# Three PSUM banks for dense products and one for heads, value differences on GpSimd, and weight casts that are deferred and kept in program order

## The chip, the cores and the metric

The kernel runs on one core of one Trainium2 chip. TensorE (PE in the profile) multiplies, VectorE (DVE), ScalarE (ACT) and GpSimd (POOL) work on tiles, and SyncE (SP) issues most DMAs. The metric is the device time of one execution in microseconds (us); lower is better.

## What is computed

A trunk of two layers on a sequence of 2048 tokens with 1024 channels, in float32:

```python
# layer 0
h = rms_norm(x, a_norm[i])
u, z = jnp.split(h @ a_w_in[i], 2, axis=-1)
# pooled: trailing means of u over 2, 4, 8, 16 tokens (one width per 256 channels) minus u
mixed = jnp.einsum('bsgc,gcd->bsgd', pooled, w_group) * scale
x = x + (mixed * jax.nn.silu(z)) @ a_w_out[i]
x = x + (p[i] @ ple_w[i]) * jax.nn.sigmoid(x @ ple_gate_w[i])
# once
k_all, v_all = jnp.split(rms_norm(x, kv_norm) @ w_kv, 2, axis=-1)
k_sh, v_sh = rms_norm(split_heads(k_all), k_norm), split_heads(v_all)
# layer 1
q, z = jnp.split(rms_norm(x, b_norm[j]) @ b_w_in[j], 2, axis=-1)
o = stick_breaking_attention(rms_norm(split_heads(q), b_q_norm[j]), k_sh, v_sh)  # 16 heads of 64, strictly causal
x = x + (o * jax.nn.silu(z)) @ b_w_out[j]
x = x + (p[i] @ ple_w[i]) * jax.nn.sigmoid(x @ ple_gate_w[i])
```

In the attention, beta = sigmoid(q·k/8), and a key's share is its beta times the product of (1 - beta) over the keys between it and the query. The kernel gets that product with a scan along the keys, and sums it against differences of neighbouring rows of v, which are therefore computed ahead ("value differences").

## The kernel before

Every operand of a product is held as a rounded high part and a low part (the rest), side by side in one tile, and a product is three matmuls: high by high, low by high, high by low. A high part is a cast or a scaled copy on ScalarE; the low part is a subtraction on VectorE or GpSimd. So each weight is loaded raw, cast (`put_split`, L183 or, where a norm's gain goes in, L189) and completed (L185, L190) before its products can start, and each activation that comes out of a product goes through `split` (L165, L166).

The tokens go in four chunks of 512. There are two streams of work. The **dense stream** (`stream`) is a generator that makes one step (three matmuls in most places) at a time: mixer, output projection (`out_steps`, whose sum with the residual is L600), the gate with its embedding (`gate_steps`: sigmoid L634, product L637, sum L638), the projections to q, k and v (`kvq`) and the gate z of layer 1 (`gate_z`). The **attention** of a chunk runs over slots of one head and one block of 512 keys: `front` (logits into psl banks, sigmoid L920, scan L924), `turn` three half-slots later (transposes into psa banks, cast L939 and low part L941) and `gather` four half-slots later (product with the value differences into a pso bank). `gather` ends a head: ScalarE copies one half of the bank out (L956), VectorE adds the other half (L957), and for every second head `gated` adds the last row (L964), multiplies by the gate on GpSimd (L965), splits and stores.

The program has three parts. `boot()` and `until((0, 0))` run the dense stream alone up to the first chunk's queries (a part called solo below: dense products rotate over the banks psd, psl and pso). Then 44 dense steps and the main loop follow: each of its turns emits one gather, turn and front, and then `fill` makes as many dense steps as a fixed rate says. Last, the projection and gate of the last chunk run alone. PSUM's eight banks are two each of psd (dense), psl (logits), pso (heads) and psa (transposes).

What sets the order: PE keeps the program's order after the mark (0, 0). On the other engines a scheduler orders instructions by its own timeline, except those that `tc.keep_in_program_order` holds behind the one traced before them. ScalarE takes its instructions strictly one after the other, so one that waits holds back those behind it. Helper `late(n, ...)` has its calls made n dense steps later (`after(n, ...)` and `store(n, ...)` likewise), and `lag` is a list of pieces that `kvq` takes up later, one at a time. Raw weights, inputs and gates share four tiles with the tag io. Nine weight pairs (`UNITS`) are in use or on their way at a time.

The value path is: `valued` scales the product (vr, L690), stores it, loads it back shifted by one row (vs); `differences` subtracts (L707, GpSimd), casts the high part (vv, L710, ScalarE), makes the low part (L711, VectorE) and stores both to DRAM (vd), from where a head's tile is loaded (L898). The path of q and k is: `keyed` scales (qs, L718), squares (sqq, L720), reduces (L723), and a piece in `lag` transposes and splits (hl, L737 to L739). A head's query tile qb is qa with its halves swapped, two copies on ScalarE (L887).

Of the kernel before, what the change touches and what calls it, by code (L numbers as in the profile page):

```python
# [37 lines left out]
def trunk_kernel(ctx, tc, x, p, a_norm, wu_t, wz_a, w_group, a_scale, a_w_out, kv_norm, w_kv,  # L38
# [90 lines left out]

    io = flat("io", 4)  # L130
    tmp_ = lambda nm: pool.tile([P, HALO + W5], F32, tag="tmp", name=nm, bufs=6)
# [47 lines left out]
    held = deque()  # L179

    def put_split(pr, raw, kts, gain):
        if gain is None:
            A.copy(out=pr[:, 0], in_=raw)  # L183
            state["lo"] += 1
            (G if state["lo"] % 3 and not state["boot"] else V).tensor_tensor(out=pr[:, 1], in0=raw, in1=f(pr[:, 0]), op=ALU.subtract)  # L185
            return
        for i, kt in enumerate(kts):
            g = gain[:, kt : kt + 1]
            booted(A.activation(out=pr[:, 0, i], in_=raw[:, i], func=AF.Identity, scale=g))  # L189
            booted(V.scalar_tensor_tensor(out=pr[:, 1, i], in0=raw[:, i], scalar=g, in1=f(pr[:, 0, i]),  # L190
                                          op0=ALU.mult, op1=ALU.subtract))

    def unit(key, src, kts, n, gain, keep):
        kk = len(kts)
        pr = pool.tile([P, 2, kk, n], F32R, tag="wpair", name="wpair", bufs=UNITS)
        if key in once:
            nc.sync.dma_start(out=f(pr), in_=once[key])
            return pr, kts
        raw = io("wraw").rearrange("q (k n) -> q k n", k=kk)
        booted(nc.sync.dma_start(out=raw, in_=src[:, kts[0] : kts[-1] + 1]))  # L200

        def finish():
            put_split(pr, raw, kts, gain)
            if keep:
                store(70, out=once[key], in_=f(pr))

        if keep:
            once[key] = scratch(f"once{len(once)}", [P, 2, kk, n])
        if state["boot"]:
            later.append(finish)  # L210
        else:
            finish()
        return pr, kts

# [65 lines left out]
    def product(ps, us, acts, c0, back):  # L280
        n = len(acts)
        i = 0
        for u, kts in us:
            for e, kt in enumerate(kts):
                hi, lo = (u[:, l, e, c0 : c0 + P] for l in range(2))
                T.matmul(ps, hi, acts[kt][:, 0], start=(i == 0), stop=False)
                yield
                T.matmul(ps, hi, acts[kt][:, 1], start=False, stop=False)
                yield
                i += 1  # L290
                T.matmul(ps, lo, acts[kt][:, 0], start=False, stop=(i == n))
                if back and e == len(kts) - 1:
                    give_back()
                yield

    def product2(pss, us, acts):
# [3 lines left out]
        for part, back in ((us[:-1], False), (us[-1:], True)):  # L300
            for k in range(2):
                for u, kts in part:
                    for e, kt in enumerate(kts):
# [184 lines left out]


    def silu(ps, rb):  # L490
        zr, sg = tmp("zr"), tmp("sg")
        V.tensor_tensor(out=zr, in0=ps, in1=rb, op=ALU.mult)
        A.activation(out=sg, in_=zr, func=AF.Sigmoid)
        G.tensor_tensor(out=zr, in0=zr, in1=sg, op=ALU.mult)
        return zr
# [150 lines left out]
    for j in (0, 2):  # L646
        STEPS += [(j, kt) for kt in range(4)]
        STEPS += [(j + i, kt + 4 * (1 - i)) for kt in range(4) for i in (1, 0)]
        STEPS += [(j + 1, kt) for kt in range(4, KT)]

    def kvq(s, kind, b):
        ck = chunk[s]
        us = take(KT)
        banks, early = {}, []
        for j, kt in STEPS:
            tk = slice(j * P, (j + 1) * P)
            if kt == 0:
                banks[j] = dense()
            u = us[kt][0]
            for xh, wh in ((0, 0), (1, 0), (0, 1)):  # L660
                T.matmul(banks[j], ck["x2"][kt][:, xh, tk], u[:, wh, 0], start=(kt == 0 and xh == wh),
# [11 lines left out]
            if "r2" not in ck:  # L673
# [32 lines left out]
    def differences(s, b, j, vr, vs):  # L706
        G.tensor_tensor(out=vs, in0=vs, in1=vr, op=ALU.subtract)  # L707
        vs = vs.rearrange("q (h d) -> q h d", d=HD)
        vv = t4("vv").rearrange("q l (h d) -> q (l h d)", d=HD).rearrange("q (h l d) -> q h l d", l=2, d=HD)
        late(10, lambda: A.copy(out=vv[:, :, 0, :], in_=vs),  # L710
             lambda: V.tensor_tensor(out=vv[:, :, 1, :], in0=vs, in1=f(vv[:, :, 0, :]), op=ALU.subtract))  # L711
        store(22, out=vd[s][b][:, :, j, :].rearrange("h q n -> q h n"),
              in_=f(vv).rearrange("q h e d -> q h (e d)"))
# [54 lines left out]
    def gate_z(s):  # L768
        ck = chunk[s]

        def put(o, zr):
            sg = tmp("sg")
            A.activation(out=sg, in_=zr, func=AF.Sigmoid)
            G.tensor_tensor(out=zr, in0=zr, in1=sg, op=ALU.mult)
            store(20, out=zd[s][o], in_=zr)

        first = []
        if "r2" in ck:
            ck["rb2"] = bcast(ck["r2"], "y")
        else:  # L780
            us = take(4)
# [148 lines left out]

    def turn(st, kt):
        j0 = kt if st["diag"] else 0
        pt = bank("psa", "psa")
# [9 lines left out]
    def gather(st, kt):  # L943
        cs = slice((kt if st["diag"] else 0) * P, W5)
        if st["diag"] and kt == 0:
            st["o"].append(bank("pso", "pso"))
        if st["last"] and kt == 1 and st["h"] % 2:
            st["zt"] = io("zt")
            nc.sync.dma_start(out=st["zt"], in_=zd[st["c"]][st["h"] // 2])
        po, at, vv = st["o"][0], st["at"].pop(kt), st["v"]  # L950
        T.matmul(po[:, cs], vv[:, kt, :], at[:, 0, cs], start=(st["diag"] and kt == 0), stop=False)
        T.matmul(po[:, cs], vv[:, kt, :], at[:, 1, cs], start=False, stop=(st["last"] and kt == 3))
        if st["last"] and kt == 3:
            half, os, c, h2 = st["h"] % 2, st["os"], st["c"], st["h"] // 2
            mine, other = slice(half * HD, (half + 1) * HD), slice((1 - half) * HD, (2 - half) * HD)
            A.copy(out=os[mine], in_=po[other])  # L956
            V.tensor_tensor(out=os[mine], in0=po[mine], in1=os[mine], op=ALU.add)  # L957
            if half:
                gated(c, h2, os, st["zt"])

    def gated(c, h2, os, zt):
# [4 lines left out]
        pr = t4("op")  # L966
        split(pr, os, G)
        if (c, h2) == (NSUB - 1, KT - 1):
            last["pair"] = pr
        else:  # L970
            store(20, out=od[c][h2], in_=f(pr))

# [33 lines left out]
    begin(0)  # L1006
    for _ in range(44):
        next(run)
    owed = 0.0
    count = 0  # L1010
# [113 lines left out]
```

## Time and profile before

| | us |
|---|---|
| median of 3 runs | 2738.69 (2737.61 to 2740.13) |
| the profiled execution | 2737.53 |
| its span, first to last instruction | 2735.7 |
| TensorE's weight loads, busy (beside matmuls) | 2248.6 |
| DMA engines, mean rate over the span | 247 GB/s |
| dense matmuls into psd, two largest groups, busy | 563.1 and 555.6 |

The span's page is from the profiled execution. Its rows by line give busy time, the mean of one instruction in ns, and the idle time just before them with what ended it. The rows of waits give the engine, the instruction that waited, after "<-" the one that released it, and then the total, the count and the longest in us. A row of the timeline starts with the start time, then the duration, and in brackets the idle time before with its releaser. The rows that matter are in the prediction.

### The profile page before, as it was taken

To read this page: it belongs to the slowest core of one execution; us is meant where nothing else is said; L and a number is where in the kernel's file an instruction comes from. 1 tells how busy PE (TensorE), PEld (TensorE's weight loads), DVE (VectorE), ACT (ScalarE), POOL (GpSimd) and SP (SyncE) were. 2 spreads that over 40 slices of the span, in tenths; PEclk is the share of its full clock that TensorE was granted. 3 is DMA by queue.
4 is the path that set the end of the run, shared out by engine and by line. 5 is a ranking of instruction groups with operands and counts; after the bars stand their busy time and mean duration, and the time that the engine had idled before them with its cause. 6 is when DMAs were issued, how large, how long until landed. Compare 5 with 4: busy or idle time off the path is not lost.

```text
span 2735.7 us, 38014 instructions
## 1 busy us (share of the span) xinstructions
PE 2688.5 (98%) x13406; PEld 2248.6 (82%) x13406; DVE 1786.0 (65%) x2303; ACT 1307.9 (48%) x2606; POOL 845.6 (31%) x681
## 2 busy tenths in 40 slices
PE   9999989999999999999999999999999999999999
PEld 7878778888787888888878888888888888888887
DVE  6736454644355866665568878766778778787742
ACT  5335553334556434564554445554565445444431
POOL 1345543324533423373333212232222102011102
PEclk9999999999999999999999999999999999999999
DMA  7789878676889878689796565677586666657545
GB/s 267 267 280 353 293 245 284 205 256 235 284 317 321 288 234 282 227 294 360 244 324 203 198 220 178 231 274 235 173 268 211 233 208 205 208 198 249 192 156 183
DMA packets 304410, 675.81 MB, mean 247 GB/s; under 512 B 46430, under 2 KB 79198, under 8 KB 304220
## 3 DMA queue, kind: packets, MB, share of 16 engines
q1 hardware_dynamic: 303644, 672.59, 72.0%
q8 instruction: 106, 1.74, 0.3%
q10 hardware_dynamic: 576, 0.79, 0.1%
q14 instruction: 84, 0.69, 0.1%
HBM read 485.05 MB, written 188.22 MB: 246 GB/s over the span
## 4 chain that ended last, share of the span: by engine, by line
PE 80%; DMA 5%; DVE 3%; ACT 2%; POOL 2%; issue 2%; SPq 1%; ACTq 0%; DVEq 0%; POOLq 0%
PE psd L47 53%; PE pso L47 9%; PE psl L47 9%; PE psa L51 8%; DVE pp L924 1%; PE pst L51 1%; DMA xin<-in_x_dram 1%; DMA vs<-vraw 1%; DMA wraw<-in_w_kv_dram 1%; DVE at L941 1%; SPq L66 1%; DMA wpair<-once 1%; DMA wraw<-in_gate_a_dram 1%; POOL rq L158 0%; DVE us L508 0%
## 5 line engine op out<-in xcount | busy, mean ns | idle before, releaser
L924 DVE TENSOR_TENSOR_SCAN pp<-pp,floor 128x512 f32<-128x512 f32 (+3 forms) x640 | 748.0, 1204 | 6.0 <-ACT pp L920 4.4
L941 DVE TENSOR_TENSOR at<-psa,at 128x512 fp32r<-128x512 f32 (+3 forms) x640 | 361.5, 605 | 344.8 <-ACT at L939 343.2
L47 PE MATMUL psd<-wpair,x 128*128 128x512 f32 x2304 | 563.1, 395 | 7.0 <-ACT qs L718 3.3
L47 PE MATMUL psd<-x,wpair 128*128 128x512 f32 x2304 | 555.6, 392 | 8.9 <-ACT sg L634 4.0
L939 ACT CAST at<-psa 128x512 fp32r<-128x512 f32 (+3 forms) x640 | 302.8, 524 | 533.8 <-PE psa L51 531.6
L47 PEld LDWEIGHTS psd<-x,wpair 128*128 128x128 f32 x2304 | 432.4, 189 | 104.0 <-ACT sg L634 6.1
L47 PEld LDWEIGHTS psd<-wpair,x 128*128 128x128 f32 x2304 | 427.1, 189 | 97.7 <-ACT qs L718 4.7
L47 PE MATMUL psd<-xp,wpair 128*128 128x512 f32 x1536 | 362.4, 391 | 3.0 <-DMA wpair<-once 1.4
L47 PEld LDWEIGHTS psd<-xp,wpair 128*128 128x128 f32 x1536 | 286.0, 188 | 64.9 <-DMA wpair<-once 1.9
L47 PE MATMUL pso<-at,vv 128*128 128x512 f32 (+3 forms) x1280 | 314.2, 365 | 6.7 <-DVE at L941 4.4
L920 ACT ACTIVATE pp<-psl 128x512 f32<-128x512 f32 (+3 forms) x640 | 316.1, 550 | 2.6 <-PE psl L47 2.1
L51 PE MATMUL psa<-ident,pp 128*128 128x128 f32 x2176 | 291.9, 274 | 0.8 <-ACT rby L366 0.8
L47 PEld LDWEIGHTS pso<-at,vv 128*128 128x128 f32 x1280 | 231.3, 188 | 58.5 <-DVE at L941 7.8
L51 PEld LDWEIGHTS psa<-ident,pp 128*128 128x128 f32 x2176 | 253.0, 141 | 29.5 <-ACT rby L366 1.0
L47 PE MATMUL psl<-kk,qa 128*128 128x512 f32 (+3 forms) x640 | 257.3, 407 | 0.0
L47 PE MATMUL psl<-kk,qb 128*128 128x512 f32 (+3 forms) x640 | 233.5, 365 | 6.0 <-ACT qb L887 6.0
L47 PE MATMUL psd<-og,wpair 128*128 128x512 f32 x744 | 182.2, 391 | 2.1 <-DVE os L957 1.4
L47 PE MATMUL psd<-mp,wpair 128*128 128x512 f32 x768 | 179.3, 390 | 0.0
L47 PEld LDWEIGHTS psd<-mp,wpair 128*128 128x128 f32 x768 | 143.8, 188 | 30.1
L47 PEld LDWEIGHTS psd<-og,wpair 128*128 128x128 f32 x744 | 138.8, 188 | 32.8 <-DVE os L957 1.8
L965 POOL TENSOR_TENSOR os<-os,zt 128x512 f32<-128x512 f32 x32 | 50.5, 1577 | 346.1 <-ACT os L964 264.7
L627 POOL TENSOR_TENSOR xj<-x 128x512 f32<-128x512 f32 x64 | 106.7, 1671 | 141.7 <-DVE sg L638 133.7
(121 smaller groups left out, 2825.7 us busy)
## 6 DMA issues: line engine op xcount, KB each, us to landing
wpair<-once SPq DMA_DIRECT2D x468, 512.0 KB, 5.1
once<-wpair SPq DMA_DIRECT2D x116, 512.0 KB, 5.8
kk<-kd SPq DMA_DIRECT2D x160, 256.0 KB, 3.7
vv<-vd SPq DMA_DIRECT2D x160, 256.0 KB, 3.9
wpair<-wf SPq DMA_DIRECT2D x48, 512.0 KB, 6.2
once<-kp SPq DMA_DIRECT2D x36, 512.0 KB, 5.5
qd<-hl SPq DMA_DIRECT2D x64, 256.0 KB, 4.4
qa<-qd SPq DMA_DIRECT2D x64, 256.0 KB, 4.5
```

The source lines that it names most:

```text
L47: return held_in_order(nc.tensor.matmul(*a, **k))
L51: return held_in_order(nc.tensor.transpose(*a, **k))
L66: after(n, lambda: nc.sync.dma_start(**k))
L627: G.tensor_tensor(out=xj, in0=f(x1[o][:, 0]), in1=f(x1[o][:, 1]), op=ALU.add)
L920: A.activation(out=pp[:, r0:], in_=ps[:, :w], func=AF.Sigmoid, scale=-1.0)
L924: V.tensor_tensor_scan(out=pp[:, r0:][:, ::-1], data0=pp[:, r0:][:, ::-1], data1=least, initial=1.0 if st["diag"] else st["carry"][j], op0 ...
L939: A.copy(out=at[:, 0, cs], in_=pt[:, cs])
L941: return lambda: V.tensor_tensor(out=at[:, 1, cs], in0=pt[:, cs], in1=f(at[:, 0, cs]), op=ALU.subtract)
L965: G.tensor_tensor(out=os, in0=os, in1=zt, op=ALU.mult)
```

## The change

- **Banks.** psd gets three banks and pso one. In the solo part dense products rotate over psd, psl, pso, psd, psl, psd.
- **Head copies.** ScalarE copies out both halves of a head's bank (the new tile is own, line 986 of the changed kernel), and VectorE adds from SBUF.
- **Value differences.** The high part is a copy on GpSimd and the low part a subtraction there, both six steps later (before: ten); the store is 24 steps later (before 22).
- **Weight casts.** After the boot part, a raw weight's cast is made five steps after its load was issued, or when a product first needs it, or when its io tile is to be used again (`settle`); and every such cast, with the kept ones (kp), stays in program order on ScalarE.
- **Sigmoids of the z gates** come five steps later (`gated_late`).
- **Order of steps.** Of the first chunk's first projection, two row blocks go weight by weight (`FIRST_STEPS`). The broadcast of the second norm goes into `lag` for chunks 1 to 3. The load of a head pair's gate zt goes from `gather` to `turn`. A head pair's split is 12 steps later and its store at 34. The first head's qb copies come after 24 of the 44 steps, in place of the first slot.

```diff
-    io = flat("io", 4)
+    io_ = flat("io", 4)
+    ring = deque([None] * 4, maxlen=4)
+
+    def io(nm, owner=None):
+        if ring[0] is not None:
+            settle(ring[0])
+        ring.append(owner)
+        return io_(nm)
...
-        return psum.tile([P, W5], F32, tag=tag, name=nm)
+        return psum.tile([P, W5], F32, tag=tag, name=nm, bufs={"psd": 3, "pso": 1}.get(tag, 2))
...
-        return bank(("psd", "psl", "pso")[state["turn"] % 3], "psd")
+        return bank(("psd", "psl", "pso", "psd", "psl", "psd")[state["turn"] % 6], "psd")
...
+    held_split = tc.keep_in_program_order
+
     def put_split(pr, raw, kts, gain):
         if gain is None:
-            A.copy(out=pr[:, 0], in_=raw)
+            held_split(A.copy(out=pr[:, 0], in_=raw))
...
-            booted(A.activation(out=pr[:, 0, i], in_=raw[:, i], func=AF.Identity, scale=g))
+            held_split(A.activation(out=pr[:, 0, i], in_=raw[:, i], func=AF.Identity, scale=g))
...
         else:
+            unsplit[id(pr)] = finish
+            after(5, lambda: settle(pr))
+        return pr, kts
+
+    unsplit = {}
+
+    def settle(pr):
+        finish = unsplit.pop(id(pr), None)
+        if finish:
             finish()
-        return pr, kts
...
+    def gated_late(zr, sg):
+        n = 0 if state["solo"] else 5
+        late(n, lambda: A.activation(out=sg, in_=zr, func=AF.Sigmoid))
+        after(n, lambda: G.tensor_tensor(out=zr, in0=zr, in1=sg, op=ALU.mult))
+        if not n:
+            pass_time(0)
...
+    FIRST_STEPS = [(j, kt) for kt in range(KT) for j in range(2)] + STEPS[16:]
...
+                if s:
+                    lag.append((time["now"] + 20, lambda: ck.update(rb2=bcast(ck["r2"], "y"))))
...
-        late(10, lambda: A.copy(out=vv[:, :, 0, :], in_=vs),
-             lambda: V.tensor_tensor(out=vv[:, :, 1, :], in0=vs, in1=f(vv[:, :, 0, :]), op=ALU.subtract))
-        store(22, out=vd[s][b][:, :, j, :].rearrange("h q n -> q h n"),
+        after(6, lambda: G.tensor_copy(out=vv[:, :, 0, :], in_=vs))
+        after(6, lambda: G.tensor_tensor(out=vv[:, :, 1, :], in0=vs, in1=f(vv[:, :, 0, :]), op=ALU.subtract))
+        store(24, out=vd[s][b][:, :, j, :].rearrange("h q n -> q h n"),
...
+        if st["last"] and kt == 0 and st["h"] % 2:
+            st["zt"] = io("zt")
+            nc.sync.dma_start(out=st["zt"], in_=zd[st["c"]][st["h"] // 2])
...
+            own = tmp("own")
             A.copy(out=os[mine], in_=po[other])
-            V.tensor_tensor(out=os[mine], in0=po[mine], in1=os[mine], op=ALU.add)
+            A.copy(out=own[mine], in_=po[mine])
+            V.tensor_tensor(out=os[mine], in0=own[mine], in1=os[mine], op=ALU.add)
...
-        split(pr, os, G)
+        split(pr, os, G, 12)
...
-    for _ in range(44):
+    for i in range(44):
         next(run)
+        if i == 24:
+            active[0]["q"][2]()
```

VectorE's order at the end of the first chunk's output projection, before: L600 adds the residual to a product (the eighth of this projection is xr_1951), L185 completes a weight, L166 is an activation's low part. Numbers behind names are tile numbers.

```order
L600 TENSOR_TENSOR xr_1861<-psd_1902,xr_1861 128x512
L166 TENSOR_TENSOR x1_1954<-xr_1861,x1_1954 128x512
L185 TENSOR_TENSOR wpair_1933<-wraw_1934,wpair_1933 128x512
L600 TENSOR_TENSOR xr_1896<-psd_1957,xr_1896 128x512
L185 TENSOR_TENSOR wpair_2009<-wraw_2010,wpair_2009 128x512
L600 TENSOR_TENSOR xr_1951<-psd_1990,xr_1951 128x512
L166 TENSOR_TENSOR x1_2040<-xr_1951,x1_2040 128x512
```

And now (L626 is the former L600, L195 the former L185, L174 the former L166):

```order
L626 TENSOR_TENSOR xr_1859<-psd_1900,xr_1859 128x512
L174 TENSOR_TENSOR x1_1952<-xr_1859,x1_1952 128x512
L195 TENSOR_TENSOR wpair_1933<-wraw_1934,wpair_1933 128x512
L626 TENSOR_TENSOR xr_1894<-psd_1955,xr_1894 128x512
L626 TENSOR_TENSOR xr_1949<-psd_1989,xr_1949 128x512
L174 TENSOR_TENSOR x1_2038<-xr_1949,x1_2038 128x512
L195 TENSOR_TENSOR wpair_2009<-wraw_2010,wpair_2009 128x512
```

The last sum, now xr_1949, and the low part of its split stand ahead of weight 2009's low part, no longer behind it.

ScalarE's order ahead of the first head's swapped query, before: L710 are casts of value differences, L189 weight casts, L718 and L720 a projection's scaled rows and their squares, L887 the two copies to qb.

```order
L189 ACTIVATE wpair_3821<-wraw_3822,gains_106 128x512
L189 ACTIVATE wpair_3832<-wraw_3833,gains_106 128x512
L710 CAST vv_3767<-vs_3706 128x8x64
L189 ACTIVATE wpair_3843<-wraw_3844,gains_106 128x512
L189 ACTIVATE wpair_3854<-wraw_3855,gains_106 128x512
L718 ACTIVATE qs_3862<-psd_3792,r_2674 128x512
L720 ACTIVATE sqq_3864<-qs_3862 128x512
L189 ACTIVATE wpair_3876<-wraw_3877,gains_106 128x512
L189 ACTIVATE wpair_3884<-wraw_3885,gains_106 128x512
L718 ACTIVATE qs_3905<-psd_3817,r_2674 128x512
L720 ACTIVATE sqq_3907<-qs_3905 128x512
L887 COPY qb_3813<-qa_3812 64x512 x2
```

And now (L199 is the former L189, L749 and L751 the former L718 and L720, L915 the former L887):

```order
L751 ACTIVATE sqq_3782<-qs_3780 128x512
L199 ACTIVATE wpair_3821<-wraw_3822,gains_106 128x512
L199 ACTIVATE wpair_3832<-wraw_3833,gains_106 128x512
L199 ACTIVATE wpair_3843<-wraw_3844,gains_106 128x512
L749 ACTIVATE qs_3860<-psd_3791,r_2657 128x512
L751 ACTIVATE sqq_3862<-qs_3860 128x512
L199 ACTIVATE wpair_3854<-wraw_3855,gains_106 128x512
L915 COPY qb_3812<-qa_3811 64x512 x2
L199 ACTIVATE wpair_3878<-wraw_3879,gains_106 128x512
L199 ACTIVATE wpair_3884<-wraw_3885,gains_106 128x512
L749 ACTIVATE qs_3903<-psd_3816,r_2657 128x512
```

The copies to qb passed two weight casts and a pair of qs and sqq, and the cast of value differences ahead of them left ScalarE.

ScalarE's order in the solo part, where the second half of the values' weights is cast, now: L397 copies a norm's sums (the former L377), L768 and L769 copy and cast transposed keys (the former L737 and L738), L721 scales values (the former L690). Before, the casts of these two weights (wpair_3593 and wpair_3618 there) stood ahead of all of these rows.

```order
L397 COPY ss_3549<-pst_3544 128x4
L768 ACTIVATE hl_3577<-pst_3572 128x512
L721 ACTIVATE vr_3654<-psd_3558,r_2657 128x512
L721 ACTIVATE vr_3699<-psd_3588,r_2657 128x512
L769 CAST hl_3577<-hl_3577 128x512
L768 ACTIVATE hl_3602<-pst_3597 128x512
L769 CAST hl_3602<-hl_3602 128x512
L199 ACTIVATE wpair_3592<-wraw_3593,gains_106 128x512
L199 ACTIVATE wpair_3617<-wraw_3618,gains_106 128x512
```

The two weight casts went behind them.

More of the change, by code (lines that the diff above doesn't have):

```diff
@@ L198, in unit @@
             return pr, kts
-        raw = io("wraw").rearrange("q (k n) -> q k n", k=kk)
+        raw = io("wraw", pr).rearrange("q (k n) -> q k n", k=kk)
         booted(nc.sync.dma_start(out=raw, in_=src[:, kts[0] : kts[-1] + 1]))
@@ L492, in silu @@
         V.tensor_tensor(out=zr, in0=ps, in1=rb, op=ALU.mult)
-        A.activation(out=sg, in_=zr, func=AF.Sigmoid)
-        G.tensor_tensor(out=zr, in0=zr, in1=sg, op=ALU.mult)
+        gated_late(zr, sg)
         return zr
@@ L654, in kvq @@
         banks, early = {}, []
-        for j, kt in STEPS:
+        for j, kt in STEPS if "r2" in ck else FIRST_STEPS:
             tk = slice(j * P, (j + 1) * P)
@@ L772, in put @@
             sg = tmp("sg")
-            A.activation(out=sg, in_=zr, func=AF.Sigmoid)
-            G.tensor_tensor(out=zr, in0=zr, in1=sg, op=ALU.mult)
-            store(20, out=zd[s][o], in_=zr)
+            gated_late(zr, sg)
+            store(24, out=zd[s][o], in_=zr)
         first = []
-        if "r2" in ck:
-            ck["rb2"] = bcast(ck["r2"], "y")
-        else:
+        if "r2" not in ck:
             us = take(4)
@@ L970, in gated @@
         else:
-            store(20, out=od[c][h2], in_=f(pr))
+            store(34, out=od[c][h2], in_=f(pr))
     slots = [(c, h, kc) for c in range(NSUB) for h in range(NH) for kc in range(c, -1, -1)]
```

6 lines of the change are left out of this document (3 added, 3 removed).

## The prediction

> **What bounds the kernel now.** I read the summary of busy time first, then the granted clock, then what TensorE waited for, then the timeline at its long waits.
>
> ```profile
> PE 2688.5 (98%) x13406; PEld 2248.6 (82%) x13406; DVE 1786.0 (65%) x2303; ACT 1307.9 (48%) x2606; POOL 845.6 (31%) x681
> core 0: 2735.7 us, clock 0.996
> ```
>
> TensorE is busy 98% of the span, and the change removes none of its products. So there are 2735.7 - 2688.5 = 47.2 us of idle time to win, and (1 - 0.996) x 2735.7 = 10.9 us that a clock below full speed cost: 58 us together, 2.1%. Anything that the change does to the other engines counts only through these.
>
> ```profile
> PE psl L47 <- ACT qb L887: 6.0, 1, 6.0
> PE psd L47 <- ACT sg L634: 5.1, 5, 1.9
> PE pso L47 <- DVE at L941: 4.4, 5, 1.4
> PE psd L47 <- ACT qs L718: 3.3, 2, 2.3
> PE psd L47 <- ACT x L165: 3.3, 1, 3.3
> PE psd L47 <- DVE sg L637: 2.4, 4, 1.1
> PE psd L47 <- ACT wpair L189: 2.3, 3, 1.8
> PE pst L51 <- DVE at L941: 2.2, 1, 2.2
> PE pso L47 <- ACT vv L710: 2.2, 1, 2.2
> PE psa L51 <- ACT rby L366: 0.8, 1, 0.8
> ```
>
> The idle time lies in a few dozen waits. Each long one is followed by slow matmuls, as the windows around four of them show (length, busy time of the five engines, then the clock, DMA share and GB/s):
>
> ```profile
> 180.00:188.00 8.00, 4.66 (x13) 2.86 (x11) 2.68 (x4) 3.09 (x5) 3.23 (x4) 0.79 0.96 316
> 331.00:337.00 6.00, 4.42 (x13) 3.37 (x14) 3.31 (x5) 3.58 (x6) 4.31 (x5) 0.73 1.01 393
> 375.00:385.00 10.00, 4.01 (x14) 3.16 (x13) 8.14 (x14) 7.59 (x14) 4.49 (x4) 0.66 0.83 252
> 733.00:740.00 7.00, 4.75 (x18) 3.71 (x18) 2.14 (x5) 2.18 (x7) 0.78 (x1) 0.76 0.96 359
> ```
>
> The clock missing there is 8 x 0.21 = 1.7, 6 x 0.27 = 1.6, 10 x 0.34 = 3.4 and 7 x 0.24 = 1.7 us. I count 1.6, 1.6, 1.5 and 1.6 as lost beside the wait; in the third window, more than half falls into the 6.0 us of waiting, where a slow clock costs nothing. [...]
>
> **The change part by part.**
>
> *a) Third bank.* The waits for sg L634, qs L718 and sg L637 are a product that finds both psd banks unread: 5.1 + 3.3 + 2.4 = **10.8 us**, none over 2.3. A third bank gives the reader one more product's time.
>
> ```profile
> 171.37 9.00 PE L47 MATMUL psd<-x,wpair 128*128 128x512 f32 x39
> 181.03 0.62 ACT L183 CAST wpair<-wraw 128x512 fp32r<-128x512 f32 x1 [2.39 <-DMA wraw<-in_gate_a_dram]
> 181.68 0.69 DVE L185 TENSOR_TENSOR wpair<-wraw,wpair 128x512 fp32r<-128x512 f32 x1 [8.18 <-ACT wpair L183]
> 182.28 0.68 DVE L600 TENSOR_TENSOR xr<-psd,xr 128x512 f32<-128x512 f32 x1
> 183.00 0.62 ACT L165 CAST x<-xr 128x512 fp32r<-128x512 f32 x1 [1.36 <-DVE xr L600]
> ```
>
> A matmul takes 9.00/39 = 0.231 us, a product of eight channel blocks by three 5.5 us: more than twice the longest wait. All 10.8 go; next in line there is the weights' arrival.
>
> *b) Residual sum.* The same rows show the wait of 3.3 us at 183.67: VectorE stood 8.18 us before a weight's low part, whose cast waited for its DMA, while the sum L600 that TensorE needed stood behind it. In the order now the sum passes that low part. What remains ahead of the x cast is 0.68 + 0.62, and the weight's DMA is no longer in the chain. **3.3 + 1.6 = 4.9 us** go; if the x cast were still caught behind one pinned weight cast, 2.4 + 0.6 of it would stay.
>
> *c) First head's query.*
>
> ```profile
> 373.99 0.62 ACT L710 CAST vv<-vs 128x512 fp32r<-128x512 f32 x1 [3.76 <-POOL vs L707]
> 378.36 0.72 ACT L189 ACTIVATE wpair<-wraw,gains 128x512 fp32r<-128x512 f32 x1 [0.65 <-DMA wraw<-in_w_kv_dram]
> 380.34 1.24 ACT L887 CAST qb<-qa 64x512 fp32r<-64x512 f32 x2
> ```
>
> ScalarE reached qb at 380.34; TensorE wanted it at 381.63 - 6.0 = 375.6. The cast vv ahead of it (0.62 and 3.76 of waiting) has left ScalarE; two weight casts (2 x 0.72 and 0.65 of waiting), a qs and a sqq (about 0.65 each) stand behind it now. That is 7.8 us earlier, 1.8 more than needed. **6.0 + 1.5 = 7.5 us**.
>
> *d) Casts vv off ScalarE.*
>
> ```profile
> 733.81 0.62 ACT L710 CAST vv<-vs 128x512 fp32r<-128x512 f32 x1 [0.72 <-POOL vs L707]
> L710 ACT CAST vv<-vs 128x512 fp32r<-128x512 f32 x32 | 20.0, 625 | 35.3 <-POOL vs L707 28.6 <-DMA kd<-hl 4.1 <-DMA od<-op 2.5
> L711 DVE TENSOR_TENSOR vv<-vs,vv 128x512 fp32r<-128x512 f32 x32 | 26.3, 822 | 48.5 <-ACT vv L710 45.0 <-DMA wraw<-in_w_kv_dram 3.5
> L739 POOL TENSOR_TENSOR hl<-hl 128x512 fp32r<-128x512 f32 x64 | 85.7, 1345 | 148.2 <-ACT hl L738 147.6 <-DMA xin<-in_x_dram 0.2
> L501 POOL COPY ub<-halo 128x16 f32<-128x16 f32 x32 | 16.6, 518 | 0.0
> ```
>
> ScalarE stood 35.3 us before these 32 casts. One such place is the wait at 735: the casts of at were queued behind vv, 2.2 us and 1.6 of clock, **3.8 us**; the wait for rby (0.8) goes as its transposes are taken up early. The 2.2 us named vv L710 I leave in: that product reads a vv tile which a DMA fetches (7.1 us in that stretch, in a row further down), and the cast is only the last event seen. For GpSimd each pair costs a subtraction of 1.345 (a row of the same shape and kind) and a copy between 0.518 (a short copy) and 1.345 (a two-input operation of full size); I take 1.2, nearer to the full size: 32 x 2.5 = 81 us on an engine that is idle 69%, against 26.3 us less on VectorE. [...] The price is that a vd tile is stored about 1.5 us and two steps later; each is needed a chunk's half later.
>
> *e) One bank for heads.*
>
> ```profile
> 2189.53 1.10 PE L47 MATMUL pso<-at,vv 128*128 128x512 f32 x4
> 2190.66 0.58 ACT L956 COPY os<-pso 64x512 f32<-64x512 f32 x1 [2.72 <-PE pso L47]
> 2194.67 0.98 PE L47 MATMUL pso<-at,vv 128*128 128x512 f32 x4
> ```
>
> Between the last product of a head and the first of the next lie 2194.67 - 2190.63 = 4.0 us here, about the smallest gap in the trace. The first copy starts at once and takes 0.58; the second adds 0.58, and the bank is free after some 1.2 us. ScalarE pays 64 x 0.58 = 37 us more and loses 20.0 with vv, of 1428 idle: no cost by itself. Nine of 64 heads have other rows between the two copies. One (head 15 of the second chunk) has six, and the bank comes about 0.5 us late; if one of those waits for a DMA, 3. **Plus 0.5.**
>
> *f) Weights in the solo part.* The order puts the first two casts of the values' second half behind ss, two hl copies, two vr and two hl casts.
>
> ```profile
> L737 ACT ACTIVATE hl<-pst 128x512 f32<-128x512 f32 x32 | 18.7, 593 | 14.8 <-PE pst L51 9.7 <-issue 3.7 <-DMA kd<-hl 1.3
> L690 ACT ACTIVATE vr<-psd,r 128x512 f32<-128x512 f32 x32 | 21.9, 689 | 22.2 <-PE psd L47 19.8 <-POOL vs L707 2.0
> L738 ACT CAST hl<-hl 128x512 fp32r<-128x512 f32 x64 | 39.4, 620 | 1.1
> L189 ACT ACTIVATE wpair<-wraw,gains 128x512 fp32r<-128x512 f32 x72 | 51.4, 721 | 50.3 <-PE psd L47 19.2 <-DMA wraw<-in_w_kv_dram 14.2 <-DMA wraw<-in_b_w_q_dram 12.1
> ```
>
> That is 0.15 (ss, four columns, an estimate) + 2 x 0.59 + 2 x 0.69 + 2 x 0.62 + 0.72 = 4.7 us after the last transposed product; TensorE gets there 0.8 us after it, waits 3.9 and pays 1.6 of clock: **plus 5.5**. The wait for L189 that stood near there (2.3, with 1.6 of clock in the window at 331) goes: **minus 3.9**.
>
> *g) Boot and rest.* Casts in the boot part are pinned behind a small copy: I put the start at **plus 1.5** (0 to 3; the nearest row is one cast's 0.6 to 0.7 a few times over). Reordering of 2,000 instructions makes waits that no row shows; I charge **plus 3**, about a tenth of what goes, with 0 and 10 as ends. The later z sigmoids, od stores and the earlier zt load move work that nobody waited for, each by a few steps, and I cost them at nothing: their readers come dozens of steps later.
>
> **The sum.** Gone: 10.8 + 4.9 + 7.5 + 3.8 + 0.8 + 3.9 = 31.7. Added: 0.5 + 5.5 + 1.5 + 3 = 10.5. Net 21.2, from the profiled execution's 2737.5 (1.2 below the median shown, 1.8 above its span): **2716.3 us**.
>
> **Rivals.**
>
> *Held casts block ScalarE (slower).* A pinned cast whose raw weight has not landed holds every sigmoid and cast of at behind it, and TensorE has two banks of cover there. Some 60 such casts fall into the main loop. Five steps hide at least 5 x 3 x 0.23 = 3.5 us of a landing, about 6 with attention between.
>
> ```profile
> wpair<-once SPq DMA_DIRECT2D x468, 512.0 KB, 5.1
> vv<-vd SPq DMA_DIRECT2D x2, 256.0 KB, 7.1
> ```
>
> The first row is the median of the program's largest group, hidden; the second, from a full stretch around 1400, is not. If 15 of the 60 wait 2 us each with TensorE behind them, that costs 30 us: 2716.3 + 30 = 2746. It decides from 0.35 us a cast. For it speaks that L189 waited 26.3 us for DMAs already; against it, that those waits hardly reached TensorE (2.3).
>
> *The pinned casts keep b, c and d alive (no change).* The sums and qb move ahead of two weight casts, but others still stand ahead, now in fixed order. Then 16.2 us stay: 2732.5, and with the upper end of the unknown waits (7 more) 2739; I take 2735.
>
> *GpSimd slows VectorE.*
>
> ```profile
> 844.68 2.29 DVE L924 TENSOR_TENSOR_SCAN pp<-pp,floor 128x512 f32<-128x512 f32 x1
> L924 DVE TENSOR_TENSOR_SCAN pp<-pp,floor 128x512 f32<-128x512 f32 x448 | 609.7, 1390 | 4.9 <-ACT pp L920 3.4
> ```
>
> This scan ran beside a GpSimd product and took 0.9 more than the mean. With 64 more GpSimd operations, two thirds beside a busy VectorE, that is 64 x 0.65 x 0.9 = 37 us, 11 more than the low parts free. If the 4.4 us of waits for at L941 double and half as much clock goes with them, the time is 2723. [...]
>
> *Cleaner than charged.* Without the 10.5 that I add, 2706.
>
> **How the numbers follow.** Forecast 0.48, GpSimd 0.12, cleaner 0.12: faster 0.72. Stays alive: 0.13, of it all within 0.2%, 5.5 us, about what a measurement of this kernel can tell from no change. Held casts: slower 0.15. The range reaches from a little below the clean case, 2702, to just over the upper end of no change, 2743; I leave out 0.05 below and 0.13 above.
>
> **What would show it.** In the profile after: no psd wait on sg or qs; no wait of 3 us at about 183 and 375; a new one of about 4 us near 350 named wpair; pso waits on own rare; the window at 735 at full clock. ScalarE idle before its weight casts on DMA far above 26 us, with TensorE waits on at or pp after them, would prove the forecast wrong.

## The result

| | us |
|---|---|
| before, median of 7 runs | 2738.95 (2737.61 to 2740.99) |
| changed, median of 7 runs | 2727.91 (2725.93 to 2732.27) |
| ratio, 95% interval | 0.9963 [0.9953, 0.9973] |
| the changed kernel's profiled execution | 2730.71 |

The change makes the kernel 11.0 us faster, 0.4%. The forecast was 22.4 us below the median shown before it (2716.3). The direction and the range were right; the gain is half of what was forecast.

The page's summary of the changed kernel and its core:

```profile
PE 2687.5 (98%) x13406; PEld 2251.0 (82%) x13406; DVE 1775.4 (65%) x2271; ACT 1321.7 (48%) x2638; POOL 915.6 (34%) x745
core 0: 2728.9 us, clock 0.995
```

TensorE's work is the same, its idle time fell from 47.2 to 41.4 us, and the clock is a little lower (0.995 for 0.996). What TensorE waited for in the changed kernel (L199 is the weight cast of before's L189, L972 the low part L941, L173 the cast L165):

```profile
PE psd L47 <- ACT wpair L199: 9.8, 5, 3.5
PE pso L47 <- DVE at L972: 7.5, 6, 2.6
PE psd L47 <- ACT ple L173: 4.5, 1, 4.5
PE pst L51 <- DVE at L972: 2.1, 3, 1.4
PE psd L47 <- DMA wpair<-once: 2.0, 1, 2.0
...
PE pst L51 <- DVE qs L756: 1.6, 2, 0.8
PE psd L47 <- DVE ul L351: 1.4, 3, 0.7
PE psd L47 <- ACT own L986: 1.3, 1, 1.3
PE psd L47 <- DVE sg L663: 1.1, 1, 1.1
...
PE psa L51 <- ACT rby L386: 0.8, 1, 0.8
```

Nearly every wait that the change was to remove is gone from the list: qb, sg on ScalarE, qs L718, x L165, the transposes at 735. Of sg on VectorE, 1.1 of 2.4 us is left. The wait for rby went from its place at 1233, but one of the same length stands at 674. New are waits for weight casts (2.3 before, 9.8 now) and one of 4.5 us for the embedding.

TensorE's program is nearly the same in both kernels, so the start of its n-th matmul can be compared. The steps in that difference, between the two profiled executions, give a ledger. It contains the slow clock behind the long waits (in the changed kernel 0.50 from 192 to 196, 0.74 from 361 to 367 and 0.73 from 850 to 855), and is of one execution each.

| place (us) | forecast | measured |
|---|---|---|
| sum behind a weight's low part, 183 | -4.9 | -4.4 |
| weight cast, 332 | -3.9 | -3.1 |
| first head's query, 375 to 390 | -7.5 | -7.7 |
| casts of at behind vv, 735 | -3.8 | -3.7 |
| head product behind vv, 1405 | 0 | -4.1 |
| psd banks and rby, many places | -11.6 | -17.8 |
| **gone** | **-31.7** | **-40.8** |
| boot, to 80 | +1.5 | +3.0 |
| embedding, 191 | 0 | +6.1 |
| weights in the solo part, 345 to 375 | +5.5 | +11.1 |
| weight of the values, 850 | 0 | +5.6 |
| one bank for heads | +0.5 | 0 |
| all else | +3.0 | +8.4 |
| **added** | **+10.5** | **+34.2** |

The net, -6.6, is that of the profiled executions, which differ by 6.8; the median of the seven runs lies 2.8 below the changed kernel's. The row of many places has one step that isn't a bank's: 1.7 at 439, where TensorE had waited for a weight's DMA. So the steps that remove were sized well or too small, and the steps that add were sized at a third of what they are.

ScalarE's timeline of the changed kernel in the solo part, with rows of VectorE and TensorE beside it:

```profile
346.98 0.62 ACT L173 CAST xp<-xin 128x512 fp32r<-128x512 f32 x1 [6.37 <-DMA xin<-in_x_dram]
...
348.56 1.32 ACT L199 ACTIVATE wpair<-wraw,gains 128x512 fp32r<-128x512 f32 x2
...
359.23 0.62 ACT L769 CAST hl<-hl 128x512 fp32r<-128x512 f32 x1
359.76 2.55 ACT L199 ACTIVATE wpair<-wraw,gains 128x512 fp32r<-128x512 f32 x4
360.51 4.67 DVE L200 SCALAR_TENSOR_TENSOR wpair<-wraw,gains,wpair 128x512 fp32r<-128x512 f32 x4 [6.88 <-ACT wpair L199]
360.53 5.53 PE L47 MATMUL psd<-wpair,x 128*128 128x512 f32 x16 [3.55 <-ACT wpair L199]
...
370.10 1.96 ACT L199 ACTIVATE wpair<-wraw,gains 128x512 fp32r<-128x512 f32 x3 [7.79 <-DMA wraw<-in_b_w_q_dram]
...
370.88 2.41 PE L47 MATMUL psd<-wpair,x 128*128 128x512 f32 x5 [1.86 <-ACT wpair L199]
```

The wait at 360 (3.55 us) is the forecast one: four casts stand behind hl and vr. Those before and behind it were not forecast. At 348 the casts stand behind the cast of an input that had just arrived after 6.37 us of waiting. At 370 ScalarE had stood 7.79 us for a raw weight. When its load was issued says why. These are SyncE's last loads of that projection's raw weights, in the kernel before and in the changed one:

```profile
354.21 0.84 SPq L200 DMA_DIRECT2D wraw<-in_b_w_q_dram  x1
```

```profile
359.44 3.06 SPq L66 DMA_DIRECT2D kd<-hl  x4
362.60 1.94 SPq L66 DMA_DIRECT2D vraw<-vr  x2
...
365.14 1.74 SPq L210 DMA_DIRECT2D wraw<-in_b_w_q_dram  x3
```

Loads that had been out by 355 were issued together at 365, about when VectorE was through with the low parts behind the casts of 359.76 (360.51 + 4.67 = 365.2) and let go of their raw tiles. A cast that comes late keeps its raw tile, of which there are four, and a later load can't have it. But SyncE has no wait for a tile at these three loads: it was busy with stores that stand ahead of them in its order. So this view alone doesn't show that the tiles are the cause; pinned_ppt below, with more of them, does.

### The profile page after: what moved, and what is told of

It reads as the page before. It is cut to its first block, busy times and chain, and to the rows that moved or that the text cites. A ratio compares the mean times of both kernels' runs of the same rounds, so it can differ in the third digit from the quotient of the medians.

```text
span 2728.9 us, 38048 instructions
## 1 busy us (share of the span) xinstructions
PE 2687.5 (98%) x13406; PEld 2251.0 (82%) x13406; DVE 1775.4 (65%) x2271; ACT 1321.7 (48%) x2638; POOL 915.6 (34%) x745
## 4 chain that ended last, share of the span: by engine, by line
PE 54%; DVE 2%; issue 0%; ACT 0%; DVEq 0%; ACTq 0%
PE psd L47 32%; PE pso L47 8%; PE psl L47 7%; PE psa L51 7%; PE pst L51 1%; DVE pp L952 1%; DVE us L534 0%; DVE at L972 0%; DVE ple L174 0%; DVE ub L528 0%; DVE us L541 0%; ACT own L986 0%; DVE os L987 0%; ACT os L985 0%; PE pst L47 0%
## 5 line engine op out<-in xcount | busy, mean ns | idle before, releaser
L972 DVE TENSOR_TENSOR at<-psa,at 128x512 fp32r<-128x512 f32 (+3 forms) x640 | 361.7, 604 | 364.0 <-ACT at L970 362.4
L47 PEld LDWEIGHTS psd<-wpair,x 128*128 128x128 f32 x2304 | 429.2, 190 | 102.2 <-ACT wpair L199 11.6
```

Of the source, the lines that this page charges most:

```text
L47: return held_in_order(nc.tensor.matmul(*a, **k))
L972: return lambda: V.tensor_tensor(out=at[:, 1, cs], in0=pt[:, cs], in1=f(at[:, 0, cs]), op=ALU.subtract)
```

## The experiments

Each time is a median, and its ratio is to runs of the kernel before on the same chip; the experiments ran on four chips, on which the kernel before has medians of 2738.2 to 2740.5. Places in us are those of the profiled executions, one of each kernel. The first four were to tell whether the weights' lost time is the fixed order (theory P) or the five steps of delay (theory H), and how much the banks give alone.

**no_pin.**

```diff
-            held_split(A.copy(out=pr[:, 0], in_=raw))
+            A.copy(out=pr[:, 0], in_=raw)
...
-            held_split(A.activation(
+            booted(A.activation(
```

> The changed kernel, in which only the weight casts after boot are no longer kept in program order on ScalarE; they are still made five steps late. Theory P (the pin is what costs): the weight waits of the solo part, +2.7 at 349, +4.7 at 360, +2.9 at 371 and +6.2 for the embedding at 191 us, mostly go, and the time falls from 2727.9 to about 2714. Theory H (the late cast holds a raw tile, so the next raw load is issued late): the loads of the queries' weights still start only at about 365, the waits stay, 2726 to 2730. If the pin is what keeps the sums and the first query ahead, waits come back instead: above 2732.

Measured: 2727.79 (2725.9 to 2736.55, 10 runs), ratio 0.9966 [0.9956, 0.9976]. The time is the one that theory H gave, but the trace bears out P up to 381 us: the last loads of the queries' weights are out at 354.34 again, the steps at 349 to 371 are gone, and TensorE is 12 us ahead of the changed kernel at 381. Of these, 3.7 are from boot, where the edit frees the casts without a gain too. But the median is that of the changed kernel. In the profiled execution, the fastest of the ten, 7 of the 12 are lost again, on balance, between 384 us and the end, in part in waits for qs (5.4 us in all, 1.6 in the changed kernel); waits for low parts of at are the same (7.7 and 7.5). So the order costs in the solo part. That it pays behind it isn't shown.

**no_defer.**

```diff
-            unsplit[id(pr)] = finish
-            after(5, lambda: settle(pr))
+            finish()
```

> The changed kernel, in which a weight's cast is written at once after its load again, but still kept in program order. Theory H: raw tiles come free as before, the loads of the queries' weights are issued from about 340 instead of 365, the waits at 349 to 371 (10.3 us) and at 191 (6.2) go, about 2712 to 2716. Theory P: casts that wait for their data now stand earlier in ScalarE's fixed order and hold more behind them: 2730 or more, with sums of idle time before weight casts on DMA above the 55 us of the changed kernel.

Measured: 2730.64 (2727.12 to 2731.56, 6 runs), ratio 0.9967 [0.9955, 0.9978]. The queries' loads are still issued late (three of them from 360.20 on), so theory H as it was put, with the delay of five steps as the cause, falls. The time is the one that theory P gave, and ScalarE's idle time before weight casts put down to raw loads is 89 us in all, against 71 in the changed kernel.

**solo_plain.**

```diff
-    held_split = tc.keep_in_program_order
+    def held_split(ins, gain=True):
+        if not state["solo"] or (gain and state["boot"]):
+            tc.keep_in_program_order(ins)
...
+        elif state["solo"]:
+            finish()
```

> The changed kernel, with weight casts in the parts where the dense stream runs alone neither late nor kept in order, as before the change; in the main loop both stay. If the missing gain was lost to the handling of weight casts in these parts, by either of the two theories, it comes to 2711 to 2716: the 3 us of boot, 6.2 at 191 and about 5 to 10 of the 10.3 at 349 to 371 go. If it was lost to something else there (the bank rotation, the order of the first projection), it stays at 2725 to 2730.

Measured: 2724.06 (2723.67 to 2726.58, 4 runs), ratio 0.9948 [0.9934, 0.9963]. Boot's 3 us are gone (-0.9 against the kernel before at 80 us) and the steps at 349 to 371 too, but the wait at 183 is back (3.9), the one for a weight cast at 334 has 3.5 us (1.8 in the kernel before), and the weight at 850 stays. Between the two outcomes: 4 of the 12 to 17 expected.

**banks_only.**

```diff
+        return psum.tile([P, W5], F32, tag=tag, name=nm, bufs={"psd": 3, "pso": 1}.get(tag, 2))
...
+        return bank(("psd", "psl", "pso", "psd", "psl", "psd")[state["turn"] % 6], "psd")
...
+            own = tmp("own")
             A.copy(out=os[mine], in_=po[other])
+            A.copy(out=own[mine], in_=po[mine])
+            V.tensor_tensor(out=os[mine], in0=own[mine], in1=os[mine], op=ALU.add)
```

> The kernel before, with only the banks (psd three, pso one, the rotation of six in the solo part) and the two copies of a head's bank. By the forecast's terms: 10.8 us of psd waits go and 0.5 comes, from 2738.95 to about 2728.6; the waits at 183 (3.3), 375 (6.0) and 735 (2.2) are still there. If the third bank brings nothing that another engine doesn't take back, 2736 to 2739; if the waits at 183, 375 and 735 were the bank's as well, below 2722.

Measured: 2733.94 (2730.73 to 2738.06, 10 runs), ratio 0.9981 [0.9971, 0.999]: 4.2 us, not 10.3. TensorE's waits in this kernel:

```profile
PE psl L47 <- ACT qb L887: 6.5, 2, 6.2
PE psd L47 <- DMA wpair<-once: 5.8, 5, 2.6
PE pso L47 <- DVE at L941: 5.5, 3, 2.8
PE psd L47 <- ACT wpair L189: 3.7, 3, 2.7
PE pso L47 <- DMA vv<-vd: 3.4, 1, 3.4
PE pst L51 <- DVE qs L725: 2.8, 1, 2.8
```

The bank waits went from the list, but for 1.1 us of sg on VectorE. What came late next was data: weights by DMA (2.6 before, 5.8 now), weight casts (2.3, 3.7), a head's vv (the wait at 1405, 2.2 before under the name of its cast, 3.4 now). In the kernel before, a wait of 2.3 us for qs at 846 covered the arrival of the values' last raw weights; without it, TensorE waits 0.7 us for their casts at 844 and 2.8 for qs at 850.

The expectation kept the waits at 183 and 735, and most of both is gone here:

```profile
180.70 0.50 PE L47 MATMUL psd<-x,wpair 128*128 128x512 f32 x1 [0.74 <-ACT x L165]
...
733.04 0.62 PE L51 MATMUL pst<-ident,r 128*128 128x128 f32 x4 [0.61 <-DVE at L941]
```

At 183 VectorE's order is that of before; the weight ahead of the sum was cast 3 us earlier (178.05, before 181.03). At 735 the casts of at stand ahead of the second cast vv on ScalarE, no longer behind it.

The next four: the value differences, the weights' part by itself, the raw tiles, and the stores that share the DMA at 850.

**vv_back.** The value differences as before the change, in the changed kernel (the change's two `after(6, ...)` lines undone, and the store at 22).

> The changed kernel with the value differences' high parts on ScalarE and low parts on VectorE again, as before (ten steps late, store at 22). By the forecast's step d the 3.7 us near 735 come back, by the trace also the 4.1 near 1405 and some of the wait for the first head's query: 2734 to 2740. If GpSimd's extra work slows VectorE (the rival), the waits of head products for the low parts at L972 (7.5 us) fall to about 4.4 as before and the time falls to 2723 to 2726.

Measured: 2745.19 (2740.47 to 2748.63, 10 runs), ratio to before 1.0014 [1.0000, 1.0028]; 17 us above the changed kernel's median, or 16 when each is taken against the kernel before on its own chip (+4.7 and -11.0), and above both expectations. The rival of GpSimd slowing VectorE falls: waits for L972 are 6.8 here and 7.5 in the changed kernel. Neither the wait at 735 nor that for the first head's query came back. The loss against the changed kernel lies in three places, 4.7 us at 767, 6.8 at 1266 and 6.7 at 1405, with what the matmuls behind the waits took longer (four head products 1.79 us behind the wait at 1266, 1.09 in the changed kernel at 1403). A row of TensorE's waits here, and one of ScalarE's:

```profile
PE pso L47 <- ACT own L986: 7.9, 2, 5.0
```

```profile
ACT vv L741 <- POOL vs L738: 30.5, 9, 8.9
```

The place at 1266:

```profile
1264.24 0.62 ACT L741 CAST vv<-vs 128x512 fp32r<-128x512 f32 x1 [2.65 <-POOL vs L738]
...
1265.30 0.56 ACT L986 COPY own<-pso 64x512 f32<-64x512 f32 x1
...
1265.91 1.79 PE L47 MATMUL pso<-at,vv 128*128 128x512 f32 x4 [4.97 <-ACT own L986]
```

A cast vv in fixed order waits for GpSimd, the copy out of the single head bank stands behind it, and the next head's products behind that. The third place is a wait for a head's vv itself (3.8, by DMA). So with one head bank, the value move keeps these waits away. What it is worth with two, or with casts that aren't held, no run shows.

**weights_only.** The kernel before with `settle`, the ring, the five steps and `held_split` as in the change.

> The kernel before with only the weights' part of the change: casts after boot five steps late, all in program order, and settled before use. If the pin costs what the trace of the changed kernel shows (3 in boot, 11 at 349 to 371, the embedding 6, minus 4.4 at 183 and 3.1 at 332), the time is 2742 to 2752. By the forecast's own sizes (plus 1.5, plus 5.5, minus 4.9, minus 3.9) it is 2734 to 2738.

Measured: 2748.74 (2746.14 to 2755.28, 8 runs), ratio 1.0036 [1.0023, 1.005]. Alone, the weights' part makes the kernel slower by 8.2 us, as the trace's sizes say and not the forecast's.

**solo_ppt** (from solo_plain).

```diff
     def io(nm, owner=None):
+        if state["solo"] and not state["boot"]:
+            return ppt(nm)
```

> The kernel solo_plain, in which raw weights and embeddings of the parts that run alone (after boot) use the eight scan tiles, which are free then, in place of the four shared ones. If loads are late there for want of a tile, they are issued earlier, the waits at 183 (3.9) and near 334 go, and the time falls by 4 to 8 to 2716 to 2720. If the DMA engines' rate sets when a weight lands (share 0.9 to 1.0 from 190 to 380 us), it stays within 2 of 2724.

Measured: 2707.09 (2705.29 to 2708.73, 4 runs), ratio 0.9879 [0.9863, 0.9895]: 17 us below solo_plain's median, more than expected. What TensorE still waited for, cut to the largest and the weights' rows:

```profile
PE pso L47 <- DVE at L978: 7.8, 6, 2.6
PE psd L47 <- DMA wpair<-once: 2.2, 1, 2.2
PE pst L51 <- DVE at L978: 2.0, 3, 1.4
...
PE psd L47 <- ACT wpair L203: 1.1, 1, 1.1
```

And what SyncE's queue waited for at the loads of raw weights, in the kernel before and in this one:

```profile
SPq L200 <- DVE wpair L190: 49.8, 29, 10.1
```

```profile
SPq L214 <- DVE wpair L204: 32.0, 16, 6.9
```

In the kernel before, SyncE stood 49.8 us before raw loads for a low part to be done, that is for a raw tile to come free. This row was there to be read before the prediction. Between 80 and 380 us, with low parts of all weights counted, it is 58 us in the kernel before, 52 in the changed one, 57 in solo_plain and 23 here. With more tiles the loads go out early, and the DMA engines' rate isn't what bound them: their mean share from 180 to 390 us is 0.86 here and 0.89 in solo_plain.

**store_late.** solo_plain with `store(100, ...)` for `store(70, ...)`.

> The kernel solo_plain with the stores of split weights 100 steps after the cast instead of 70. If the wait of about 5 us near 843 to 850 is for a raw weight that shares full DMA engines with these stores (1.02 to 1.05 busy there), it shrinks by 2 to 5 as the stores move behind 850, and the time falls to 2719 to 2723, unless the stores meet other loads later. If that landing has another cause, the wait stays: 2723 to 2727.

Measured: 2723.21 (2720.39 to 2724.1, 4 runs), ratio 0.9939 [0.9921, 0.9957]: within the noise of solo_plain's 2724.06. The step at 850 is smaller by 1.3 us at most, so these stores are not its main cause. What delays that landing stays open.

The last four: whether the fixed order costs by held tiles or by itself, and what the tiles give alone.

**pinned_ppt** (the changed kernel; `wide` is a second ring, of eight).

```diff
     def io(nm, owner=None):
+        if state["solo"] and not state["boot"]:
+            if wide[0] is not None:
+                settle(wide[0])
+            wide.append(owner)
+            return ppt(nm)
```

> The changed kernel, weight casts late and in program order everywhere as in it, with the eight scan tiles for raw weights and embeddings in the parts that run alone after boot. If the fixed order costs there because a late cast keeps a raw tile and the next load waits for the tile, the price is gone with more tiles: 2706 to 2712, near solo_ppt (2707.1). If it costs because casts stand behind other work on ScalarE, whatever the tiles, the waits at 349 and 360 stay (2.7 and 4.9) and boot's 3: 2714 to 2720.

Measured: 2719.73 (2716.74 to 2722.03, 4 runs), ratio 0.9933 [0.9918, 0.9947]. It looks like the second outcome, but the place is another: from 180 to 390 us this kernel gains 18.5 us on the kernel before, as solo_ppt does, and the steps at 349 to 371 are gone. The changed kernel loses 1.9 there, so the tiles are worth 20 us in it. The loss is in boot. Two of TensorE's rows there, and the windows of boot (the clock is the third number from the end):

```profile
26.28 1.05 PE L47 MATMUL pst<-ones,sq 128*128 128x1 f32 x8 [2.02 <-ACT sq L456]
...
31.56 1.63 PE L47 MATMUL psd<-xp,wpair 128*128 128x512 f32 x3
```

```profile
24.00:32.00 8.00, 5.98 (x33) 5.31 (x32) 0.68 (x3) 5.15 (x10) 0.00 (x0) 0.82 1.00 396
32.00:40.00 8.00, 8.00 (x31) 7.13 (x30) 0.00 (x0) 0.00 (x0) 0.00 (x0) 0.50 0.09 36
40.00:48.00 8.00, 8.00 (x30) 7.13 (x30) 0.62 (x2) 1.33 (x4) 1.00 (x2) 0.50 0.00 1
48.00:56.00 8.00, 8.00 (x41) 6.83 (x40) 5.21 (x12) 5.57 (x11) 1.33 (x2) 0.90 0.83 304
```

One wait of 2.0 us, and TensorE runs at half its clock for 20 us (from about 29 to 50) while it is busy all the time.

**before_ppt.** The kernel before with the eight tiles in the solo part, nothing else.

> The kernel before with those eight tiles for raw loads in the parts that run alone after boot, and nothing else. If the want of raw tiles was a bound there before the change too, the waits at 183 and 332 (3.3 and 2.3 and 1.6 of clock behind each) go, and part of the embedding's: 2728 to 2733. If four tiles were enough before and fell short only with the pin, 2736 to 2740.

Measured: 2729.4 (2727.42 to 2732.09, 7 runs), ratio 0.9965 [0.9954, 0.9976]. Four raw tiles were a bound before the change too: 9.4 us, nearly as much as the whole change brings. Of these, 8 come, on balance, between 180 and 390 us, where the tiles bring the changed kernel 20; so some 12 us is what want of tiles costs there because of the change.

**ppt_store_late.** solo_ppt with the stores at 100.

> The kernel solo_ppt with the stores of split weights 100 steps after the cast instead of 70, as a version that may beat both kernels. If the stores crowd the last raw weights near 830, 2703 to 2706; if those land in time now, as the waits of solo_ppt have it (1.1 us for weights in all), no difference: 2706 to 2709.

Measured: 2707.38 (2706.56 to 2707.74, 4 runs), ratio 0.9887 [0.9871, 0.9904]: no difference.

**pinned_ppt_boot.**

```diff
-            held_split(A.copy(out=pr[:, 0], in_=raw))
+            (A.copy if state["boot"] else lambda **k: held_split(A.copy(**k)))(out=pr[:, 0], in_=raw)
```

> The kernel pinned_ppt, but in boot the casts of weights without a gain are not kept in program order, as before the change. The trace of pinned_ppt has its whole loss against solo_ppt before 55 us: a wait of 2.0 at 26 us, then half the clock for 25 us, 12 us in all; from 180 to 375 us it gains as much as solo_ppt (20). So the theory that the fixed order costs outside boot only through held raw tiles gives 2705 to 2710 here, within 3 of solo_ppt. If the order itself costs outside boot, or the slow stretch had another cause than the pinned boot casts, it stays at 2715 to 2721.

Measured: 2709.35 (2706.79 to 2711.12, 4 runs), ratio 0.9886 [0.9869, 0.9902]. The slow stretch is gone, the clock is 1.00 from 24 to 56 us. So outside boot the fixed order, with the five steps, costs 2 to 3 us once raw tiles are plenty, and the runs of the two kernels overlap. solo_ppt beats both kernels: 33 us below the kernel before on its chip, 21 below the changed one's median.

## Why the forecast gain was twice the measured one

- **The waits that go** (steps a to d, and the wait for L189 in f). They went where the forecast put them, but for the wait for rby, which moved, and b, c and d within 0.5 us each. Two went further: the third bank also took short waits that the list of waits had under other names, and the wait at 1405, left in as a DMA's, went with the casts vv (it is back in vv_back).
- **Step d** had its size from one window in the kernel before, and met it at 735 (3.7 for 3.8) by luck: that wait is down to 0.6 with the banks alone, and it doesn't come back in vv_back. In the changed kernel the move is worth 16 to 17 us: at 767 and 1266 through copies of the one head bank that would stand behind vv, at 1405 through the vv itself. Step c didn't need it either: the first head's query has no wait in vv_back.
- **Step e**, one bank for heads, costs nothing that the trace of the changed kernel shows; its upper end showed only in vv_back (7.9).
- **Step f failed, in its term of plus 5.5.** It counted what stands ahead of two casts on ScalarE and found that wait (3.55 us at 360, 4.9 with the clock, for 3.9 and 5.5). It did not follow what the late casts hold: the raw tile, and through it the next loads. The whole place cost 11.1 (345 to 375). The casts are late by the fixed order, not by the five steps: without the steps the loads are still late (no_defer), without the order they are not (no_pin). That the tile is the link is shown by pinned_ppt and pinned_ppt_boot: the same fixed order, more tiles, no such waits. SyncE's own waits for low parts didn't grow by the change (58 us before, 52 now), so it is by their place in its order that the loads are late.
- **Step b's sentence "the weight's DMA is no longer in the chain" failed next.** The sum went ahead, but TensorE then waited for the embedding. Its load needs one of the same four tiles; it was issued at 184.4, two us later than before (SyncE had stood for low parts before it and the loads ahead of it), and took two us longer to land, so that its cast came at 190.5. This took back 6.1 against the 4.4 won. With more tiles the wait is gone (pinned_ppt, load issued at 176.5). Why the landing was slower is open. The rows, of SyncE in the kernel before and in the changed one, then of ScalarE and TensorE in the changed kernel:

```profile
182.40 0.33 SPq L610 DMA_DIRECT2D pin<-in_p_dram  x1
```

```profile
184.44 1.51 SPq L636 DMA_DIRECT2D pin<-in_p_dram  x2
...
190.51 1.28 ACT L173 CAST ple<-pin 128x512 fp32r<-128x512 f32 x2 [3.73 <-DMA pin<-in_p_dram]
191.18 1.22 PE L47 MATMUL psd<-ple,wpair 128*128 128x512 f32 x2 [4.47 <-ACT ple L173]
```

- **Step a's "next in line there is the weights' arrival"** named the right thing and priced it at nothing. banks_only gives 4.2 where step a minus e gives 10.3, although it also takes most of the waits at 183 and 735.
- **Step g.** Boot cost 3.0 instead of 1.5, at the end of its bounds of 0 to 3; the tenth charged for new waits was 3 and came to 8.4, inside 0 to 10. The weight at 850 (5.6) was in no term.
- **The rivals.** Held casts did block, but mostly in the solo part rather than in the main loop where the rival had put them, and through tiles rather than through sigmoids. Its sign didn't come: ScalarE's idle time before casts L199 on those two loads is 30.5 us (17.7 and 12.8), for 26.3 before. The shortage shows at the queue that issues the loads. GpSimd's extra work was as sized: its row for the copies has 818 ns and for the low parts 1510, together 2.3 us for the 2.5 estimated. It didn't slow VectorE's scan, whose mean is 1387 ns after and 1390 before.

```profile
L741 POOL CAST vv<-vs 128x512 fp32r<-128x512 f32 x32 | 26.0, 818 | 7.5 <-DMA od<-op 6.9
L742 POOL TENSOR_TENSOR vv<-vs,vv 128x512 fp32r<-128x512 f32 x32 | 48.2, 1510 | 1.1
L952 DVE TENSOR_TENSOR_SCAN pp<-pp,floor 128x512 f32<-128x512 f32 x448 | 607.3, 1387 | 4.0 <-ACT pp L948 3.2
```

What stays open: the landing near 850, the many short waits of the 8.4, and why no_pin loses behind 384 us much of what it wins before.

## What to carry to other kernels

When an instruction is moved later, follow the buffer that it frees, not only the results that it makes: here a cast that came late held one of four tiles, and the load queue behind the tile was most of the cost in that part (some 12 us from 180 to 390, against 2 to 3 of the fixed order with the five steps). The load queue's own waits showed the shortage ahead of time (49.8 us in the kernel before), and a few more tiles from a pool that is idle in that stage were worth nearly as much as the whole reordering without it (9.4 us for 11.0), and 17 us on top of it (solo_ppt below solo_plain). A removed wait is worth what is late next at that place; where that is data from memory, price its arrival (banks_only brought 4.2 us of 10.3).

## What was not expected of the hardware

One wait of 2.0 us in a stretch of products mixed with one-column matmuls was followed by half TensorE's clock from about 29 to 50 us, though it was busy throughout (pinned_ppt, 0.50 in the windows from 32 to 48); three matmuls of 512 columns took 1.63 us there, and in the changed kernel, at the same place, 0.94:

```profile
31.72 0.94 PE L47 MATMUL psd<-xp,wpair 128*128 128x512 f32 x3
```

So the same alternation ran at full clock in one kernel (1.00 in each window from 24 to 56) and stayed at half clock in the other (0.50), where the wait came first. It ends at 46.5 with nine matmuls of 512 columns in a row, and some 3 us later the full clock is back (0.90 over 48 to 56 leaves half clock to 49.6). That the one-column products are what held it down is not shown.

```profile
46.49 3.73 PE L47 MATMUL psd<-xp,wpair 128*128 128x512 f32 x9
```
